# A two-layer trunk on one core: the work between dense blocks gathered into runs, one pool of eight PSUM banks, joined inverses

## The chip, the core and the metric

The kernel runs on one core of one Trainium2 chip. The metric is device time in microseconds of one execution. The core has a matrix engine (TensorE, PE in the profile), a vector engine (VectorE, DVE), an activation engine (ScalarE, ACT), GpSimd (POOL) and SyncE (SP), which issues most transfers. Each engine takes its own instructions in order and waits on semaphores for the others.

## What is computed

A sequence of 256 tokens of width 2048 goes through two layers. Layer 0 is differential attention and a gated MLP with a depthwise convolution (ffn); layer 1 is a gated delta net and a second ffn. Cut to what matters:

```python
x = x + diff_attention(rms_norm(x, mixer_norm[0]), ...)      # 8 heads, two scores each
x = x + conv_ffn(rms_norm(x, ffn_norm[0]), ...)              # 2048 -> 2 x 5504 -> 2048
x = x + gated_deltanet(rms_norm(x, mixer_norm[1]), ...)      # 16 key heads, 32 value heads
x = x + conv_ffn(rms_norm(x, ffn_norm[1]), ...)

# inside the delta net, per head and chunk of 64 tokens
low = where(strict, einsum(k_beta, k) * decay, 0)
a_mat = low + eye(64)
u = triangular_solve(a_mat, v_beta); w = triangular_solve(a_mat, k_beta * exp(g_c))
v_new = u - w @ state;  o = q_dec @ state + qk @ v_new
```

All of it is float32 in and out.

## The kernel before

Tokens lie along the free dimension, features along the 128 partitions. A product with a weight matrix is a **dense block**: `dense` (L109) makes 256 output features from all input features in chunks of four 128-row tiles. For each chunk `weights` (L85) loads 512 KB of weights (`raw`, on SP), casts them on ACT to a rounded copy (`whi`, L98), and takes the rest on DVE (`wlo`, L99). Each tile then makes three passes on PE (L123 to L125): high by high, low by high, high by low. `dense_tok` (L178) does the same with tokens on the partitions, in passes of 512 columns (L190), in chunks of two tiles.

The **other work** (normalization, scores, transposes, the delta rule) is written as Python generators. `spawn` puts one into the list `bg`; after each chunk of a dense block `tick` (L80) advances every generator to its next `yield`. That sets a priority only: the scheduler of the program then places each instruction, by a simulated timeline of its own, where it finds it ready, so a step of other work may stand anywhere among the dense passes.

PSUM is split into two pools: `dps` with two tiles of two banks each for dense blocks (`ps`), and `mps` with four banks for the rest (`mp`).

The delta net handles its 16 key heads in four blocks of four, b = 0 to 3. Per block it runs four key projections, one value projection, two gate projections by `dense_tok` (`z`), and three more value projections; behind those come the output projections `out` of the block before. `keys` makes for each head the sum of squares (`mp<-qp,onesr`, L284), scales and exponents on ACT, the product of norms on DVE (`cv<-cv,qs`, L567), and then the products k·k and k·q (`mp<-cv`, L574 and L575), from which come `lt` and `qkt`. When all four heads are there, `invert` (L589) inverts 32x32 triangles of the whole block on DVE: a transpose to `X` (L594), 30 steps of two dependent operations (L602 and L605), and two transposes to `ttc` and `tcc` (L609, L611). `levels` (L614) joins the 32x32 inverses to 64x64 ones on PE in small tiles, in four steps, each fed by copies out of PSUM; it does so for two heads at a time, inside `group` (L670). `group` then applies the rule and makes the activations `oc` for `out`. `gates` (L784) makes the decays once, in a chain of small operations from `mp<-fold,glin` to `mp<-gt,con`.

Attention sums squares of queries and keys (`mp<-sqp,onesr`, L284), makes scores (`mp<-qkn`, L411 and L412) and weights their values.

Of the kernel before, what the change touches and what calls it, by code (L numbers as in the profile page):

```python
# [13 lines left out]
PSUM = bass.MemoryType.PSUM  # L14
DATA = mybir.DependencyInfo(mybir.DependencyClass.Sync, mybir.DependencyReason.DATA)
# [9 lines left out]
RING = 4  # L25
LNEXP = "natural_log_exp_and_others"


class Trunk:
# [8 lines left out]
    def __init__(self, ctx, tc):  # L38
        self.tc, self.nc = tc, tc.nc
        nc = self.nc  # L40
        self.bg = deque()
        self.cp = ctx.enter_context(tc.tile_pool(name="cp", bufs=1))
# [15 lines left out]
        nc.scalar.preload_act_table_set(LNEXP)  # L58
# [9 lines left out]
    def mp(self):  # L68
        return self.mps.tile([P, 512], F32, tag="mp", name="mp")

    def warm(self, n):

        p = self.mp()
        for _ in range(n):
            self.nc.tensor.matmul(p[:, :P], self.ones, self.ones, start=True, stop=True)

    def spawn(self, gen):
        self.bg.append(gen)
# [6 lines left out]
    def weights(self, ap, d, pieces=1):  # L85

        nc = self.nc
        nk, n = ap.shape[1:]

        def tile_(tag, dt, bufs, room=0, d=0):  # L90
            t = self.wp.tile([P, CK * T + room], dt, tag=tag, name=tag, bufs=bufs)
            return t[:, d:d + nk * n].rearrange("p (k n) -> p k n", n=n)

        raw, hi, lo = tile_("raw", F32, RING), tile_("whi", F32R, RING, P, d), tile_("wlo", F32R, RING, P, d)
        for i in range(pieces):
            s = slice(i * nk // pieces, (i + 1) * nk // pieces)
            self.load = nc.sync.dma_start(raw[:, s, :], ap[:, s, :])
            self.cast = nc.scalar.copy(hi[:, s, :], raw[:, s, :])  # L98
            nc.vector.tensor_tensor(lo[:, s, :], raw[:, s, :], hi[:, s, :].bitcast(F32), ALU.subtract)  # L99
        return hi, lo  # L100
# [5 lines left out]
    def banks(self):  # L106
        return self.dps.tile([P, 2, 2 * T], F32, tag="ps", name="ps")

    def dense(self, w, kt, acts, place, tiles=2):  # L109
# [3 lines left out]
        for k0, nk in self.chunks(kt, CK):  # L113
            hi, lo = self.weights(w[:, k0:k0 + nk, :], (place - GAP) % P)
            steps = [(k, c) for k in range(nk) for c in range(tiles)]
            if k0 + nk == kt:
                steps = [(k, c) for c in range(tiles) for k in range(nk)]
            for k, c in steps:
                a = acts(k0 + k)
                first, last = k0 + k == 0, k0 + k == kt - 1  # L120
                s = slice(c * P, (c + 1) * P)
                o = ps[:, c, :T]
                nc.tensor.matmul(o, hi[:, k, s], a[:, 0, :], start=first, stop=False)  # L123
                nc.tensor.matmul(o, lo[:, k, s], a[:, 0, :], start=False, stop=False)  # L124
                nc.tensor.matmul(o, hi[:, k, s], a[:, 1, :], start=False, stop=last)  # L125
# [7 lines left out]
    def twin(self, w, kt, acts, place):  # L133
# [3 lines left out]
        for k0, nk in self.first_chunks(kt):  # L137
            for k in range(k0, k0 + nk):
                acts(k)
            hi, lo = self.weights(w[:, k0:k0 + nk, :], (place - GAP) % P, 1 if k0 else nk)  # L140
# [5 lines left out]
            for l, i, k, c in steps:  # L146
                nc.tensor.matmul(pss[c // 2][:, c % 2, :T], l[:, k, c * P:(c + 1) * P], acts(k0 + k)[:, i, :],  # L147
# [8 lines left out]
    def dense_gate(self, w, kt):  # L156

        nc = self.nc
        ps = self.banks()
        n = w.shape[2]  # L160
        for k0, nk in self.chunks(kt, CK):
# [8 lines left out]
            for k in range(nk):  # L170
                a = self.h[k0 + k]
                passes = [(2 * n, both[:, k].rearrange("p i n -> p (i n)"), a[:, 0, :]), (n, both[:, k, 0, :], a[:, 1, :])]
                for m, l, r in passes if k0 + k == 0 else passes[::-1]:
                    nc.tensor.matmul(ps[:m, 0, :T], l, r, start=k0 + k == 0 and m > n, stop=k0 + k == kt - 1 and m > n)
# [3 lines left out]
    def dense_tok(self, w, kt, acts):  # L178
# [3 lines left out]
        for k0, nk in self.chunks(kt, CK // 2):  # L182
            hi, lo = self.weights(w[:, k0:k0 + nk, :], HP + LEAD)
            for k in range(nk):
                a = acts(k0 + k)
                first, last = k0 + k == 0, k0 + k == kt - 1
                for c in range(2):
                    ah, al = (a[:, i, c * P:(c + 1) * P] for i in range(2))
                    for j, (l, r) in enumerate(((ah, hi), (ah, lo), (al, hi))):
                        nc.tensor.matmul(ps[:, c, :], l, r[:, k, :], start=first and not j, stop=last and j == 2)  # L190
# [33 lines left out]
    def norm_stat(self, parts=(KD, KD), switch=False):  # L224
# [10 lines left out]
        nc.tensor.matmul(ps[:, :T], self.ones, ss, start=True, stop=True)  # L235
        for c in range(2):
            last = nc.tensor.matmul(
# [41 lines left out]
    def total(self, out, parts):  # L279

        n = len(parts)
        for i, p in enumerate(parts):
            for j in range(2):
                last = self.nc.tensor.matmul(out, self.onesr, p[:, j], start=i + j == 0, stop=i + j == n)  # L284
        return last

    def add_out(self, blk, ps, done):

        x = self.x[:, 2 * blk:2 * blk + 2, :]
        self.nc.vector.tensor_tensor(x, ps[:, :, :T], x, ALU.add)  # L290
# [5 lines left out]
    def project(self, w, kt, acts, place, done, final=False):  # L296

        n = KD // 2
        for b in range(n):
# [4 lines left out]
            for c in range(2):  # L304
                k = 2 * b + c
                self.nc.vector.tensor_tensor(self.x[:, k, :], ps[:, c, :T], self.x[:, k, :], ALU.add)
# [30 lines left out]
    def attention(self, w_first, w_qk, w_v, w_o, nh, dist_ap, ident_ap, qg, kg, lvec, sub, start, done, lambda_init):  # L337

        nc, mp = self.nc, self.mp
        with self.tc.tile_pool(name="at", bufs=1) as at:  # L340
# [9 lines left out]
            def prepare():  # L350
                for _ in range(11):
                    yield
                with self.tc.issue_after(self.load.ins):
                    nc.sync.dma_start(dist, dist_ap)
                    nc.sync.dma_start(ident, ident_ap)
                nc.vector.tensor_scalar(qgs, qg, P ** -0.5, None, ALU.mult)
                nc.vector.tensor_scalar(subs, sub, 1.0 - lambda_init, None, ALU.mult)
                for i in range(2):
# [623 lines left out]
```

## Time and profile before

| | us |
|---|---|
| median of 3 runs (lowest, highest) | 2635.81 (2635.53, 2636.52) |
| the profiled execution's own time | 2635.23 |
| its span, first to last instruction | 2633.4 |
| VectorE busy in the span | 1840.9 |
| ScalarE busy in the span | 1451.2 |
| TensorE's mean granted clock | 1.000 |

The times of one instruction are rows of the trace. Matmuls overlap, and their ends are modelled: what one costs is the distance between the starts of two that follow each other, not its own length. A float32 matmul has two records, a float32r one or a transpose has one. A row of a group gives busy time and mean time of one, then the idle time of its engine just ahead of it, with what ended that.

### The profile page before, as it was taken

How to read it: one execution, taken by the hardware profiler on the slowest of the kernel's cores; microseconds unless marked ns; L12 is line 12 of the kernel's file. 1: busy time of each engine (PE TensorE's matmuls, PEld its weight loads, DVE VectorE, ACT ScalarE, POOL GpSimd, SP SyncE). 2: the span in 40 equal slices, each digit the busy share in tenths (PEclk: the TensorE clock that was granted, in tenths of full speed). 3: DMA queues.
4: the chain of work that ended last, by engine and by line, in shares of the span. 5: the costliest groups of instructions: out<-in, count | busy, mean ns of one | idle time of the engine just before them, and what ended most of it. 6: DMA issues, size and time to landing. Idle time of an engine off the chain costs nothing.

```text
span 2633.4 us, 53599 instructions
## 1 busy us (share of the span) xinstructions
PE 2625.5 (100%) x22324; PEld 2566.1 (97%) x22324; DVE 1840.9 (70%) x2716; ACT 1451.2 (55%) x1996; POOL 92.9 (4%) x188
## 2 busy tenths in 40 slices
PE   9999999999999999999999999999999999999999
PEld 9998899999999999999989989989999999999999
DVE  7876567777777555589788688688677777776444
ACT  6665555555555444485674674674555555554333
POOL 0000000000000000011011011021000000000000
PEclk9999999999999999999999999999999999999999
DMA  7555566666666666655455365455466666666665
GB/s 247 162 175 174 156 199 195 194 193 196 194 194 194 193 193 194 193 179 193 137 184 187 125 195 169 150 184 177 138 195 194 195 194 194 194 194 199 199 202 152
DMA packets 138244, 485.34 MB, mean 184 GB/s; under 512 B 15728, under 2 KB 19088, under 8 KB 138000
## 3 DMA queue, kind: packets, MB, share of 16 engines
q1 hardware_dynamic: 137712, 481.56, 59.3%
q8 instruction: 174, 2.85, 0.4%
q14 instruction: 70, 0.57, 0.1%
q10 hardware_dynamic: 288, 0.35, 0.0%
HBM read 479.72 MB, written 2.13 MB: 183 GB/s over the span
## 4 chain that ended last, share of the span: by engine, by line
PE 99%; DVE 0%; DMA 0%; ACT 0%; issue 0%; SPq 0%; DVEq 0%
PE ps L123 27%; PE ps L124 27%; PE ps L125 27%; PE ps L190 10%; PE mp L687 2%; PE ps L147 1%; PE mp L284 1%; PE mp L575 1%; PE mp L657 0%; PE mp L651 0%; PE mp L666 0%; PE mp L574 0%; PE mp L412 0%; PE mp L442 0%; PE mp L731 0%; DMA raw<-w_first 0%
## 5 line engine op out<-in xcount | busy, mean ns | idle before, releaser
L99 DVE TENSOR_TENSOR wlo<-raw,whi 128x1024 fp32r<-128x1024 f32 (+1 forms) x905 | 1102.6, 1220 | 616.4 <-ACT whi L98 613.3
L98 ACT CAST whi<-raw 128x1024 fp32r<-128x1024 f32 (+1 forms) x905 | 944.9, 1046 | 987.3 <-PE ps L125 825.1
L123 PE MATMUL ps<-h,whi 128*128 128x256 f32 x4224 | 1171.9, 277 | 0.0
L125 PE MATMUL ps<-h,whi 128*128 128x256 f32 x4224 | 1171.7, 277 | 0.0
L124 PE MATMUL ps<-h,wlo 128*128 128x256 f32 x4224 | 1171.6, 277 | 0.0
L124 PEld LDWEIGHTS ps<-h,wlo 128*128 128x128 f32 x4224 | 793.8, 188 | 1.3
L123 PEld LDWEIGHTS ps<-h,whi 128*128 128x128 f32 x4224 | 793.7, 188 | 1.2
L125 PEld LDWEIGHTS ps<-h,whi 128*128 128x128 f32 x4224 | 793.8, 188 | 0.5
L123 PE MATMUL ps<-ac,whi 128*128 128x256 f32 x1632 | 451.2, 277 | 0.0
L124 PE MATMUL ps<-ac,wlo 128*128 128x256 f32 x1632 | 451.2, 277 | 0.0
L125 PE MATMUL ps<-ac,whi 128*128 128x256 f32 x1632 | 451.1, 277 | 0.0
L124 PEld LDWEIGHTS ps<-ac,wlo 128*128 128x128 f32 x1632 | 306.5, 188 | 0.0
L123 PEld LDWEIGHTS ps<-ac,whi 128*128 128x128 f32 x1632 | 306.5, 188 | 0.0
L125 PEld LDWEIGHTS ps<-ac,whi 128*128 128x128 f32 x1632 | 306.4, 188 | 0.0
L190 PE MATMUL ps<-whi,h 128*128 128x512 f32 x768 | 240.8, 390 | 0.0
L190 PEld LDWEIGHTS ps<-whi,h 128*128 128x128 f32 x768 | 144.2, 188 | 29.8
L190 PE MATMUL ps<-wlo,h 128*128 128x512 f32 x384 | 150.1, 391 | 0.0
L123 PE MATMUL ps<-oc,whi 128*128 128x256 f32 x512 | 143.0, 279 | 0.8 <-ACT oc L734 0.8
L125 PE MATMUL ps<-oc,whi 128*128 128x256 f32 x512 | 142.8, 279 | 0.6 <-DVE oc L735 0.6
L124 PE MATMUL ps<-oc,wlo 128*128 128x256 f32 x512 | 142.8, 279 | 0.0
L265 DVE SCALAR_TENSOR_TENSOR cv<-u,fcols,cv 128x255 f32<-128x255 f32 (+1 forms) x344 | 142.8, 477 | 0.0
L131 DVE TENSOR_TENSOR u<-ps,rstd 128x512 f32<-128x512 f32 x118 | 81.4, 690 | 36.3 <-PE ps L125 35.3
(205 smaller groups left out, 2069.2 us busy)
## 6 DMA issues: line engine op xcount, KB each, us to landing
raw<-w_up SPq DMA_DIRECT2D x344, 512.0 KB, 4.3
raw<-w_down SPq DMA_DIRECT2D x160, 512.0 KB, 3.7
raw<-w_in SPq DMA_DIRECT2D x128, 512.0 KB, 4.4
raw<-w_z SPq DMA_DIRECT2D x64, 512.0 KB, 3.9
raw<-w_out SPq DMA_DIRECT2D x64, 512.0 KB, 4.2
raw<-w_qk SPq DMA_DIRECT2D x56, 512.0 KB, 4.1
raw<-w_v SPq DMA_DIRECT2D x32, 512.0 KB, 3.7
raw<-w_o SPq DMA_DIRECT2D x32, 512.0 KB, 4.4
```

What stands on the lines that cost most here:

```text
L98: self.cast = nc.scalar.copy(hi[:, s, :], raw[:, s, :])
L99: nc.vector.tensor_tensor(lo[:, s, :], raw[:, s, :], hi[:, s, :].bitcast(F32), ALU.subtract)
L123: nc.tensor.matmul(o, hi[:, k, s], a[:, 0, :], start=first, stop=False)
L124: nc.tensor.matmul(o, lo[:, k, s], a[:, 0, :], start=False, stop=False)
L125: nc.tensor.matmul(o, hi[:, k, s], a[:, 1, :], start=False, stop=last)
L131: self.nc.vector.tensor_tensor(u, ps[:, :, :T], self.rstd.unsqueeze(1).to_broadcast([P, 2, T]), ALU.mult)
L147: nc.tensor.matmul(pss[c // 2][:, c % 2, :T], l[:, k, c * P:(c + 1) * P], acts(k0 + k)[:, i, :], start=k0 + k == 0 and l is hi and i == 0, ...
L190: nc.tensor.matmul(ps[:, c, :], l, r[:, k, :], start=first and not j, stop=last and j == 2)
L265: nc.vector.scalar_tensor_tensor(out[:, j:], u[:, :T - j], taps[n - 1 - j], out[:, j:], ALU.mult, ALU.add)
L284: last = self.nc.tensor.matmul(out, self.onesr, p[:, j], start=i + j == 0, stop=i + j == n)
L575: nc.tensor.matmul(p[:, P:384], k[:, :P], r, start=True, stop=True)
L687: nc.tensor.matmul(p[:, v, :], l(v), r[:, v, :], start=i == 0, stop=i == len(terms) - 1)
```

## The change

Four things are done.

- **Runs.** A generator may `yield RUN`. `tick` now counts; generators at a plain `yield` go on at every tick, those at `RUN` only at every `period`-th. The period is 4, one dense block of four chunks; it is 1 in attention's output projection, and 2 in the first and last block of the delta net outside the key projections. Where it is 4, all PE work that a tick issues is chained (`queue`): each matmul is ordered behind the one before it, the first behind the last dense pass, and the next dense pass behind the last of the run.
- **Banks.** One pool of eight banks, used in turn; a dense block takes two of them as two tiles, so that evictions (`merge`, `add_out`) are two operations, one for each.
- **Joined inverses.** `levels` becomes `join`: it works once for all four heads of a block, behind `invert`, and its steps are steps of runs. `group` waits until the block is joined, and until the group before has got two steps on. `keys` of a head wait for those of the head before.
- **Start and ends.** Six warm matmuls instead of nine; the first loads are cut up and spread over SP's and ACT's queues, the first weights cast on DVE; small loads of attention come at other ticks.

```diff
     def tick(self):
-        for g in list(self.bg):
-            if next(g, self) is self:
-                self.bg.remove(g)
+        self.ticks += 1
+        slot = self.ticks % self.period == 0
+        for run in (False, True):
+            self.run = run and self.period == CK
+            for task in list(self.bg):
+                if task[1] is (RUN if run else None) and (slot or not run) and task[2:] != [self.ticks]:
+                    task[1:] = [next(task[0], self), self.ticks]
+                    if task[1] is self:
+                        self.bg.remove(task)
+        self.run = False
+    def queue(self, ins):
+        if self.run or self.resume:
+            self.tc.add_manual_dep(ins.ins, self.last.ins.name, ORDER)
+            self.resume = self.run
+        self.last = ins
+        return ins
-        self.dps = ctx.enter_context(tc.tile_pool(name="dps", bufs=2, space=PSUM))
-        self.mps = ctx.enter_context(tc.tile_pool(name="mps", bufs=4, space=PSUM))
+        self.ps = ctx.enter_context(tc.tile_pool(name="ps", bufs=8, space=PSUM))
     def banks(self):
-        return self.dps.tile([P, 2, 2 * T], F32, tag="ps", name="ps")
+        return [self.bank("ps") for _ in range(2)]
     def merge(self, ps, u):
-        self.nc.vector.tensor_tensor(u, ps[:, :, :T], self.rstd.unsqueeze(1).to_broadcast([P, 2, T]), ALU.mult)
+        for c in range(2):
+            self.nc.vector.tensor_tensor(u[:, c, :], ps[c][:, :T], self.rstd, ALU.mult)
...
             def keys(hq, c, cc, b0, res):
+                while "col" not in gates or turn[0] < hq:
+                    yield
...
-                yield
-                yield
+                turn[0] = hq + 1
+                yield RUN
                 prods = []
...
-                inv += [ttc, tcc]
+                yield from join(lqs, ttc, tcc, mark)
+            def join(lqs, ttc, tcc, mark):
+                while using:
+                    yield
...
+                yield RUN
                 pp = small(32)
-                for m in range(nm):
+                for m in every:
                     for s in (0, 2):
-                        nc.tensor.matmul(pp[quad[s + 1], m, :], lview[m // 2][quad[s], m % 2, quad[s + 1]],
-                                         tcc[quad[s], m0 + m, :], start=True, stop=True)
+                        self.mm(pp[quad[s + 1], m, :], lt(m)[quad[s], quad[s + 1]],
+                                         tcc[quad[s], m, :], start=True, stop=True)
...
+                yield RUN
                 px = small(32)
...
             def group(gi, gr, lqs, mark, vt, ready, zts, acts):
-                while len(inv) < 2:
+                while mark not in joined or len(ready) < len(gr) or gi and steps.get((mark, gi - 1), 0) < 2:
                     yield
-                yield from levels(TT, Ta, [lt for lt, _ in sub], *inv, 4 * gr[0])
...
                 for op, i in plan + [("v", i) for i in range(1, hb)]:
+                    self.period = 2 if op != "k" and b in (0, nb - 1) else CK
```

Matmuls are now issued in one line of the kernel, L78, and transposes in L81, so the rows of PE are told apart by their tiles. The first place in the order is PE at b=1, from the last key's products to the first step of the join. Before, with L123 to L125 and L190 for the dense passes:

```order
L575 MATMUL mp<-cv 128x256
L666 MATMUL mp<-con,cv 128x128 x4
L190 MATMUL ps<-whi,h 128x512 x2
...
L125 MATMUL ps<-oc,whi 128x256
L630 MATMUL mp<-tcc,lt 32x32 x16
L123 MATMUL ps<-oc,whi 128x256
```

And after the change:

```order
L78 MATMUL mp<-cv 128x256
L81 MATMUL mp<-con,cv 128x128 x4
L78 MATMUL ps<-whi,h 128x512
...
L78 MATMUL ps<-whi,h 128x512
L78 MATMUL mp<-tcc,lt 32x32 x32
L78 MATMUL ps<-h,whi 128x256
```

Between the rows shown stood 528 dense passes of 256 columns and 40 of 512; now there stand 137 of 512. At b=2 there are 144, at b=0 and b=3 192 (all of 512 columns). On DVE, between `X` and `tcc`, stand all 60 operations of the 30 steps, and with them 11 casts of weights (`wlo`) at b=1 now, 12 at b=2, 15 at b=0 and b=3; before, there were 19 to 23 casts and 12 to 18 operations of convolutions.

The second place is PE at b=0, the first steps of the join. Before, 29 dense passes stood between the first step (`mp<-tcc,lt`) and the second (`mp<-ttc,pc`), and 38 from there to the third (`mp<-Ta,lt`). After the change:

```order
L78 MATMUL ps<-whi,h 128x512
L78 MATMUL mp<-tcc,lt 32x32 x32
L78 MATMUL mp<-ttc,pc 32x32
L78 MATMUL mp<-pc,TT 32x32 x8
L78 MATMUL mp<-ttc,pc 32x32 x31
L78 MATMUL mp<-pc,TT 32x32 x8
L78 MATMUL mp<-Ta,lt 64x64 x8
L78 MATMUL ps<-h,whi 128x256
```

The three steps follow each other without a dense pass.

The third place is PE at b=0, the sums of squares of the last key head and its products. Before:

```order
L190 MATMUL ps<-whi,h 128x512
L284 MATMUL mp<-qp,onesr 128x512
L190 MATMUL ps<-whi,h 128x512
...
L190 MATMUL ps<-whi,h 128x512 x2
L574 MATMUL mp<-cv 128x128
L575 MATMUL mp<-cv 128x256
```

And after the change:

```order
L78 MATMUL mp<-qp,onesr 128x512
L78 MATMUL ps<-h,whi 128x256
L78 MATMUL mp<-qp,onesr 128x512
L78 MATMUL mp<-cv 128x128
L78 MATMUL mp<-cv 128x256
```

The products stood 49 dense passes behind the second sum; now they follow it directly. In the same way the two places of the gates' chain (`mp<-fold,glin` and `mp<-gt,con`) had 192 dense passes between them and have 114, and the eight sums of the first two heads of attention, which stood in eight places, are one row, `mp<-sqp,onesr 128x512 x8`, behind the fifth dense block (480 passes).

More of the change, by code (lines that the diff above doesn't have):

```diff
@@ L25 @@
 RING = 4
+RUN = "run"
 LNEXP = "natural_log_exp_and_others"
@@ L68, in mp, with bank, mm, tr @@
     def mp(self):
-        return self.mps.tile([P, 512], F32, tag="mp", name="mp")
+        return self.bank("mp")
+    def bank(self, name):
+        return self.ps.tile([P, 2 * T], F32, tag="bank", name=name)
+    def mm(self, *args, **kwargs):
+        return self.queue(self.nc.tensor.matmul(*args, **kwargs))
+    def tr(self, *args, **kwargs):
+        return self.queue(self.nc.tensor.transpose(*args, **kwargs))
+    def queue(self, ins):
[4 more added lines that the diff above has]
+        return ins
     def warm(self, n):
@@ L74, in warm @@
         for _ in range(n):
-            self.nc.tensor.matmul(p[:, :P], self.ones, self.ones, start=True, stop=True)
+            self.mm(p[:, :P], self.ones, self.ones, start=True, stop=True)
     def spawn(self, gen):
-        self.bg.append(gen)
+        self.bg.append([gen, None])
     def tick(self):
-        for g in list(self.bg):
-            if next(g, self) is self:
-                self.bg.remove(g)
-    def weights(self, ap, d, pieces=1):
-        nc = self.nc
[L88 to L99, printed above, removed]
+        self.ticks += 1
@@ new lines, in fetch, with weights @@
+    def fetch(self, ap):
+        raw = self.part(ap, "raw", F32, RING)
+        self.load = self.nc.sync.dma_start(raw, ap)
+        return raw
+    def weights(self, ap, d, raw=None, cast=None):
+        nc = self.nc
+        raw = self.fetch(ap) if raw is None else raw
+        hi, lo = self.part(ap, "whi", F32R, RING, P, d), self.part(ap, "wlo", F32R, RING, P, d)
+        if cast:
+            cast(hi, lo)
+            return hi, lo
+        self.cast = nc.scalar.copy(hi, raw)
+        self.low = nc.vector.tensor_tensor(lo, raw, hi.bitcast(F32), ALU.subtract)
@@ L121, in dense @@
                 s = slice(c * P, (c + 1) * P)
[L122 to L125, printed above, removed]
+                o = ps[c][:, :T]
+                self.mm(o, hi[:, k, s], a[:, 0, :], start=first, stop=False)
+                self.mm(o, lo[:, k, s], a[:, 0, :], start=False, stop=False)
+                self.mm(o, hi[:, k, s], a[:, 1, :], start=False, stop=last)
             self.tick()
@@ L129, in merge, with first, cast, twin @@
     def merge(self, ps, u):
-        self.nc.vector.tensor_tensor(u, ps[:, :, :T], self.rstd.unsqueeze(1).to_broadcast([P, 2, T]), ALU.mult)
-    def twin(self, w, kt, acts, place):
+        for c in range(2):
+            self.nc.vector.tensor_tensor(u[:, c, :], ps[c][:, :T], self.rstd, ALU.mult)
+    def first(self, ap, d, raw, acts):
+        nc = self.nc
+        def cast(hi, lo):
+            for i in range(2):
+                s = slice(i * T, (i + 1) * T)
+                nc.vector.tensor_copy(hi[:, 0, s], raw[:, 0, s])
+            for k in range(raw.shape[1]):
+                acts(k)
+                if k:
+                    nc.scalar.copy(hi[:, k, :], raw[:, k, :])
+                nc.vector.tensor_tensor(lo[:, k, :], raw[:, k, :], hi[:, k, :].bitcast(F32), ALU.subtract)
+        return self.weights(ap, d, raw, cast)
+    def twin(self, w, kt, acts, place, raw, ahead):
         nc = self.nc
@@ L158, in dense_gate @@
         nc = self.nc
-        ps = self.banks()
+        ps = self.bank("ps")
         n = w.shape[2]
@@ L189, in dense_tok @@
                     for j, (l, r) in enumerate(((ah, hi), (ah, lo), (al, hi))):
-                        nc.tensor.matmul(ps[:, c, :], l, r[:, k, :], start=first and not j, stop=last and j == 2)
+                        self.mm(ps[c], l, r[:, k, :], start=first and not j, stop=last and j == 2)
             self.tick()
@@ L234, in norm_stat @@
         ps = self.mp()
-        nc.tensor.matmul(ps[:, :T], self.ones, ss, start=True, stop=True)
+        self.mm(ps[:, :T], self.ones, ss, start=True, stop=True)
         for c in range(2):
-            last = nc.tensor.matmul(
+            last = self.mm(
                 ps[:, T + c:T + c + 1], ss[:, c * P:(c + 1) * P], self.ones[:, :1], start=True, stop=True)
@@ L283, in total @@
             for j in range(2):
-                last = self.nc.tensor.matmul(out, self.onesr, p[:, j], start=i + j == 0, stop=i + j == n)
+                last = self.mm(out, self.onesr, p[:, j], start=i + j == 0, stop=i + j == n)
         return last
     def add_out(self, blk, ps, done):
-        x = self.x[:, 2 * blk:2 * blk + 2, :]
-        self.nc.vector.tensor_tensor(x, ps[:, :, :T], x, ALU.add)
+        for c in range(2):
+            x = self.x[:, 2 * blk + c, :]
+            self.nc.vector.tensor_tensor(x, ps[c][:, :T], x, ALU.add)
         if done:
@@ L522, in gdn @@
             gates = {}
+            turn, steps = [0], {}
             def lin(ps):
```

263 lines of the change are left out of this document (148 added, 115 removed).

## The prediction

> **What bounds the kernel now.** I read the page first: the busy row and the chain of work that ended last.
>
> ```profile
> PE 2625.5 (100%) x22324; PEld 2566.1 (97%) x22324; DVE 1840.9 (70%) x2716; ACT 1451.2 (55%) x1996; POOL 92.9 (4%) x188
> PE 99%; DVE 0%; DMA 0%; ACT 0%; issue 0%; SPq 0%; DVEq 0%
> ```
>
> The chain is TensorE (PE) almost from end to end, and no other engine has 1% of it. So nothing that VectorE (DVE) or ScalarE (ACT) does now ends late, and whatever makes PE wait is added to the time in full. The next view is busy time by windows: a stretch of layer 0's ffn, and the stretch in which block b=1 of the delta net inverts its matrices.
>
> ```profile
> core 0: us, PE busy (x) PEld busy (x) DVE busy (x) ACT busy (x) POOL busy (x), PEclk, DMA share, GB/s
> 700.00:800.00 100.00, 100.00 (x885) 100.00 (x884) 71.96 (x101) 55.41 (x75) 0.00 (x0) 1.00 0.64 193
> 1364.70:1430.60 65.90, 65.90 (x554) 64.76 (x553) 62.04 (x114) 32.21 (x38) 1.75 (x6) 1.00 0.57 185
> ```
>
> The dense passes of 256 columns start 100 / 882 = 0.1134 us apart (three of the 885 only reach into the window). The second row matters most: there DVE is busy 62.0 of 65.9 us. It has no slack, and PE is not held up only because nothing in PE's queue needs the inverse yet. The dense work does not change (19,312 passes of 256 columns and 1152 of 512, with 16 narrow ones), so the question is what happens between its blocks.
>
> **What the change saves.** Gathering the other work leaves 100 stretches of it between dense passes where there were 161, and 16 stretches of 32x32 and 64x64 tiles where there were 28. The timeline of PE shows what a stretch of small tiles costs to enter and leave.
>
> ```profile
> 1244.97 0.28 PE L123 MATMUL ps<-h,whi 128*128 128x256 f32 x1
> 1245.17 0.69 PE L630 MATMUL mp<-tcc,lt 32*32 32x32 f32 x32
> 1245.80 0.39 PE L124 MATMUL ps<-h,wlo 128*128 128x256 f32 x1
> 1246.02 0.28 PE L125 MATMUL ps<-h,whi 128*128 128x256 f32 x1
> ```
>
> The first small matmul starts 0.20 us behind a dense one that takes 0.113, and the dense pass behind the stretch holds its successor off for 0.22 instead of 0.113: 0.2 us for each. Twelve fewer are worth 2.4 us. A single transpose shows the price of a stretch at full size.
>
> ```profile
> 1291.47 0.28 PE L123 MATMUL ps<-h,whi 128*128 128x256 f32 x1
> 1291.59 0.27 PE L731 MATMUL mp<-con,zt 128*128 128x128 f32 x1
> 1291.82 0.28 PE L125 MATMUL ps<-h,whi 128*128 128x256 f32 x1
> ```
>
> Two dense passes and the transpose take 0.35 us, of which 0.227 is dense. The 0.12 left is hardly more than the 0.11 of a transpose among others (the row of eight below), so I put the other 49 at 0.02 each, 1 us. [...]
>
> ```profile
> 1886.00 1.04 PE L731 MATMUL mp<-con,zt 128*128 128x128 f32 x8
> 1887.89 0.38 PE L123 MATMUL ps<-oc,whi 128*128 128x256 f32 x1 [0.85 <-ACT oc L734]
> ```
>
> Here the last `out` waits for its activations, about 1.9 us with what follows; the new ends of the last block have dense passes in that place. The new start (three warm matmuls fewer, loads over two queues) and the two-part evictions I put at 1.7 us together, between 0 and 3. **Saved: 7 us, between 3 and 10.**
>
> **The joined inverse, b=1 and b=2.** The rule of a bound run is a wait: PE takes its instructions in order, and everything dense stands behind the run. In the order, the last key's products (`mp<-cv`) and the first step of the join (`mp<-tcc,lt`) had 568 dense passes between them at b=1 (528 of 256 columns, 40 of 512), 69 us. After the change there are 137 of 512 columns (144 at b=2). Their spacing, and the work of DVE that must fit:
>
> ```profile
> 1364.84 0.61 PE L190 MATMUL ps<-whi,h 128*128 128x512 f32 x2
> ...
> 1368.24 0.61 PE L190 MATMUL ps<-whi,h 128*128 128x512 f32 x2
> ```
>
> ```profile
> L99 DVE TENSOR_TENSOR wlo<-raw,whi 128x1024 fp32r<-128x1024 f32 (+1 forms) x905 | 1102.6, 1220 | 616.4 <-ACT whi L98 613.3
> L605 DVE TENSOR_TENSOR Ti<-Ti,tmp 128x30 f32<-128x30 f32 (+14 forms) x120 | 39.6, 330 | 2.3
> L602 DVE TENSOR_TENSOR tmp<-X,Ti 128x30 f32<-128x30 f32 (+14 forms) x120 | 39.4, 328 | 2.4
> L611 DVE STREAM_TRANSPOSE tcc<-Ti 128x1024 f32<-128x1024 f32 x4 | 8.7, 2185 | 0.0
> L609 DVE STREAM_TRANSPOSE ttc<-Ti 128x1024 f32<-128x1024 f32 x4 | 8.4, 2102 | 0.1
> ```
>
> Fifteen passes in 3.40 us are 0.227 us each, so PE comes to the join 137 x 0.227 = 31.1 us after the products (32.7 at b=2). DVE needs, for one inverse, (39.6 + 39.4 + 8.7 + 8.4) / 4 = 24.0 us, 1.25 for `X` (below) and some 0.7 for the negated copy of a tile of that size: 26.0. Between `X` and `tcc` its order holds 11 casts of weights (12 at b=2) of 1.22 us, 13.4 (14.6). Ahead of `X` stand the products of the last key, the copies into `Cc` and two casts:
>
> ```profile
> 1360.30 0.38 PE L574 MATMUL mp<-cv 128*128 128x128 f32 x2
> ...
> 1364.76 1.25 DVE L594 STREAM_TRANSPOSE X<-Cc 128x1024 f32<-128x1024 f32 x1 [0.61 <-POOL Cc L585]
> ```
>
> That is 4.5 us. Together 43.9 against 31.1, and 45.1 against 32.7: 12.8 and 12.4, and I take **14 at each, 28**, since the 60 steps depend on each other and the latency between them is in no group's busy time. Bounds: nothing if all casts rode in gaps of the inverse (4.5 + 26.0 are 30.5); with the 65.9 us that `X` to `tcc` took in before, 39 each.
>
> **b=0 and b=3.** Here 192 passes, 43.6 us, stand between products and join, and 15 casts: 4.5 + 26.0 + 18.3 make 48.8, a wait of 5.2, taken as 6.5 for the same latency. Behind the first step the order has the next two with no dense pass between, each fed by copies out of PSUM.
>
> ```profile
> L633 DVE COPY pc<-mp 32x256 f32<-32x256 f32 x8 | 3.3, 418 | 0.2
> ```
>
> The copies have twice the elements now; two in turn for `pc` and one for `Ta` at about 0.65 are 2 us. **17 us** for both blocks, between 4 and 40.
>
> **The gates.**
>
> ```profile
> 1112.52 0.56 PE L796 MATMUL mp<-fold,glin 128*128 128x64 f32 x4
> ...
> 1132.77 0.29 DVE L816 SCALAR_TENSOR_TENSOR gt<-gt,ga 128x32 f32<-128x32 f32 x2
> ```
>
> The chain of small operations from the fold to the last `gt` takes 20.5 us among the casts and convolutions. PE now meets its product after 114 dense passes, 12.9 us, instead of 192. It waits 7.6 us if the chain keeps its length; **6** with fewer casts in between; bounds 0 and 8.
>
> **Keys.** At b=0 the sum of squares of the last key and its products now stand next to each other; the trace shows what lies between.
>
> ```profile
> 1170.42 0.39 PE L284 MATMUL mp<-qp,onesr 128*128 128x512 f32 x1
> ...
> 1171.00 1.28 ACT L252 ACT_TABLE_LOAD   x1
> ...
> 1180.12 0.69 DVE L567 TENSOR_TENSOR cv<-cv,qs 128x512 f32<-128x512 f32 x1
> ```
>
> As it ran, 10.4 us, about half of it casts and convolutions that need not stand there; the table load and the product alone are 2.0. I take **6** at b=0 and 6 at b=3, where the same pair meets, and **4** at b=2, where two sums stand behind products whose squares are still being made: 16 us, between 6 and 25.
>
> **Attention.** All eight sums of the first two heads now stand at the end of the fifth dense block, which PE passes at about 65.9 us.
>
> ```profile
> 67.60 0.63 ACT L276 CAST sqp<-sq 128x512 fp32r<-128x512 f32 x1
> ...
> 69.05 0.68 DVE L277 TENSOR_TENSOR sqp<-sq,sqp 128x512 fp32r<-128x512 f32 x1
> ```
>
> The last of these squares is split at 69.7 us now, so 3.8 us of waiting at least; **5** with the first heads' scaling ahead of it. The transposes of `zt` that are no longer spread I put at **2**.
>
> **The clock.** PE's warm-up rows and the last window show the granted clock move.
>
> ```profile
> 1.05 4.21 PE L75 MATMUL mp<-ones 128*128 128x128 f32 x18 [1.05 <-DVE eps L50]
> 1482.62 1.05 PE L687 MATMUL mp<-w,lt 128*128 128x128 f32 x8
> 2633.60:2634.00 0.40, 0.00 (x0) 0.00 (x0) 0.00 (x0) 0.00 (x0) 0.00 (x0) 0.50 0.00 0
> ```
>
> The same shape goes at 0.23 us a record for the first 4.2 us and at half of that later, and the clock is 0.50 some 4 us after the last matmul. A wait of 4 to 7 us may drop it, one of 14 surely does, and 4 us at half rate lose 2. Nine waits are that long: between 4 and 18 us, taken as **10**. [...]
>
> **The sum.** Waits 28 + 17 + 6 + 16 + 5 + 2 = 74. Against the profiled execution's own 2635.2 us: + 74 + 10 - 7 = 2712; its time is 0.6 below the median of the runs, inside the rounding. I predict 2712 us, 2.9% slower.
>
> **Rivals.** (1) *The joined work is ready in time*: the run waits for nothing and only the savings are left, 2635 - 7 = 2628. It decides at 31 us for `X` to `tcc` and what precedes it. For it: DVE could do the inverse before the casts that stand between. Against it: the order has the casts in between, and without them 30.5 of the 31.1 us are already taken. 4%, and 2% more that smaller waits cancel the savings. (2) *Only the inverses wait* because the shorter chains are faster without the casts around them: 2635 + 45 + 5 - 7 = 2678. 7%. (3) *The ring of eight banks stops dense blocks*: a block now takes the two banks given out longest ago, and a group that still reads `os` in one of them holds up both the block and all behind it; eight groups at about 2 us are 16 more, 2728. No bank is waited for in the trace of before. 9%. (4) *The clock stays up*, 2702, 14%, or falls at each wait and the waits last longer, 2725, 14%. The forecast itself, 50%.
>
> **Range and chances.** The bounds of the long terms do not add up at one end; forecast, (3) and (4) lie within 2690 to 2735, 87%, and I keep that. Faster by over 0.2% (about what a measurement of this kernel can tell from no change): 0.04. Within it: 0.02. Slower: 0.94.
>
> **What would show it.** Right: idle time of PE ahead of `mp<-tcc,lt` of 12 to 17 us at b=1 and b=2, released by the transposes on DVE; 5 to 7 us ahead of the gates' product and of `mp<-cv` at b=0; a mean granted clock below 1.00 behind them. Wrong: `tcc` done before PE comes to the join, DVE idle in these stretches, or idle time of PE ahead of `ps` that ends with an eviction.

## The result and the profile after

| | before | after |
|---|---|---|
| median (lowest, highest), us | 2636.16 (2635.53, 2637.39) | 2724.23 (2723.21, 2725.75) |
| span of the profiled execution, us | 2633.4 | 2721.4 |
| TensorE's mean granted clock | 1.000 | 0.983 |

The ratio is 1.0335, with a 95% interval of 1.0322 to 1.0348: the kernel is 88 us slower. The page after, busy times and the chain that ended last:

```profile
PE 2648.0 (97%) x22318; PEld 2584.6 (95%) x22318; DVE 1856.9 (68%) x2903; ACT 1444.7 (53%) x1988; POOL 76.2 (3%) x188
PE 94%; DVE 4%; ACT 1%; issue 1%; DMA 0%; SPq 0%; DVEq 0%; ACTq 0%
```

PE is busy in 97% of its span instead of all of it, and DVE has appeared in the chain. PE idles 73.4 us where it idled 7.9; and it is busy 22.5 us longer with six records fewer. Two things were lost, then: time in waits, and speed. What ended PE's waits (engine and line that waits, what it waited for, us in total, times, the longest):

```profile
PE mp L78 <- DVE tcc L680: 36.3, 4, 14.5
PE mp L78 <- DVE cv L636: 10.7, 2, 6.0
PE mp L78 <- DVE gt L898: 5.8, 1, 5.8
PE mp L78 <- ACT sqp L333: 5.4, 1, 5.4
PE mp L78 <- DVE qp L334: 3.8, 2, 2.4
PE mp L78 <- ACT qp L333: 2.2, 2, 1.8
PE mp L78 <- DVE pc L712: 1.5, 2, 0.8
PE mp L78 <- DVE Ta L725: 1.2, 2, 0.6
...
PE mp L81 <- DVE zt L803: 0.7, 2, 0.6
```

These are 67.6 us, all of them ahead of `mp`, the other work; no dense block waits for a bank. More than half are the joins. Two of the four, on the timeline of PE:

```profile
1419.64 1.56 PE L78 MATMUL mp<-tcc,lt 32*32 32x32 f32 x51 [14.53 <-DVE tcc L680]
1646.22 1.92 PE L78 MATMUL mp<-tcc,lt 32*32 32x32 f32 x64 [13.27 <-DVE tcc L680]
```

The speed is seen in a table of windows, cut to the nine stretches in which the granted clock stood at half:

```profile
67.10:73.90 6.80, 3.63 (x13) 3.10 (x14) 4.58 (x9) 4.84 (x8) 0.00 (x0) 0.50 0.21 72
...
1237.80:1251.50 13.70, 11.95 (x198) 11.62 (x199) 3.42 (x6) 2.07 (x5) 5.20 (x10) 0.50 0.14 41
1408.50:1425.60 17.10, 5.96 (x83) 5.92 (x84) 10.93 (x25) 0.58 (x1) 5.67 (x13) 0.50 0.10 32
...
1865.90:1879.60 13.70, 12.12 (x199) 11.79 (x200) 3.34 (x6) 2.07 (x5) 4.17 (x9) 0.50 0.14 41
sum 92.40, PE 54.36 PEld 50.36 DVE 47.64 ACT 24.82 POOL 24.64; mean PE 6.04 PEld 5.60 DVE 5.29 ACT 2.76 POOL 2.74
```

The first number behind the length is PE's busy time. Each of the nine lies on or behind one of the long waits, and PE worked 54.4 us in them. If all of that goes at half rate, 27 us are lost. Small tiles of 32x32 took 28 ns a record at 0.50 and 17 at 1.00 in a probe (below), less than twice as long; with that for the small tiles of the join I estimate the loss at about 25. 67.6 + 25 is 92.6, against 88.1: about 4.5 us were saved elsewhere, by this account.

### The profile page after: what moved, and what is told of

Read it like the earlier page. It is cut to its first block, busy times and chain, and to the rows that moved or that the text cites. A ratio compares the mean times of both kernels' runs of the same rounds, so it can differ in the third digit from the quotient of the medians.

```text
span 2721.4 us, 53724 instructions
## 1 busy us (share of the span) xinstructions
PE 2648.0 (97%) x22318; PEld 2584.6 (95%) x22318; DVE 1856.9 (68%) x2903; ACT 1444.7 (53%) x1988; POOL 76.2 (3%) x188
## 4 chain that ended last, share of the span: by engine, by line
PE 94%; DVE 4%; ACT 1%; issue 1%; DMA 0%; SPq 0%; DVEq 0%; ACTq 0%
PE ps L78 88%; PE mp L78 5%; DVE wlo L134 1%; PE mp L81 1%; ACT whi L133 0%; DVE cv L322 0%; DVE Ti L674 0%; DVE tcc L680 0%; DVE tmp L671 0%; DMA raw<-w_in 0%; DMA raw<-w_first 0%; DVE d L624 0%; DVE ttc L678 0%; ACT L309 0%; DVE u L167 0%
## 5 line engine op out<-in xcount | busy, mean ns | idle before, releaser
L78 PE MATMUL ps<-h,whi 128*128 128x256 f32 (+1 forms) x8608 | 1486.5, 278 | 1.5 <-DVE whi L176 1.1
L78 PEld LDWEIGHTS ps<-h,whi 128*128 128x128 f32 (+1 forms) x8608 | 1306.5, 189 | 3.7 <-issue 1.3
L78 PE MATMUL ps<-h,wlo 128*128 128x256 f32 x4288 | 1181.7, 278 | 0.0
L78 PEld LDWEIGHTS ps<-h,wlo 128*128 128x128 f32 x4288 | 806.1, 189 | 1.4 <-issue 0.2
L78 PE MATMUL ps<-ac,whi 128*128 128x256 f32 x3264 | 555.9, 276 | 0.0
L78 PEld LDWEIGHTS ps<-ac,whi 128*128 128x128 f32 x3264 | 492.2, 188 | 0.0
L78 PE MATMUL ps<-ac,wlo 128*128 128x256 f32 x1632 | 450.2, 276 | 0.0
L78 PEld LDWEIGHTS ps<-ac,wlo 128*128 128x128 f32 x1632 | 306.3, 188 | 0.0
L78 PE MATMUL ps<-whi,h 128*128 128x512 f32 x768 | 242.5, 393 | 0.0
L78 PE MATMUL ps<-oc,whi 128*128 128x256 f32 x1024 | 179.0, 278 | 0.0
L78 PEld LDWEIGHTS ps<-whi,h 128*128 128x128 f32 x768 | 145.7, 190 | 31.0
L78 PEld LDWEIGHTS ps<-oc,whi 128*128 128x128 f32 x1024 | 155.7, 188 | 0.0
L78 PE MATMUL ps<-wlo,h 128*128 128x512 f32 x384 | 150.5, 392 | 0.0
L78 PE MATMUL ps<-oc,wlo 128*128 128x256 f32 x512 | 141.3, 276 | 0.0
L167 DVE TENSOR_TENSOR u<-ps,rstd 128x256 f32<-128x256 f32 x236 | 98.3, 420 | 8.3 <-PE ps L78 0.9
L78 PEld LDWEIGHTS ps<-oc,wlo 128*128 128x128 f32 x512 | 96.2, 188 | 0.0
L320 ACT ACTIVATE cv<-u,fcols 128x256 f32<-128x256 f32 x172 | 93.6, 592 | 0.0
L78 PEld LDWEIGHTS ps<-wlo,h 128*128 128x128 f32 x384 | 73.0, 190 | 15.3
L322 DVE SCALAR_TENSOR_TENSOR cv<-u,cols,cv 128x255 f32<-128x255 f32 (+2 forms) x192 | 82.8, 475 | 1.3 <-ACT cv L318 1.1
```

Source lines behind the costliest of these rows:

```text
L78: return self.queue(self.nc.tensor.matmul(*args, **kwargs))
L167: self.nc.vector.tensor_tensor(u[:, c, :], ps[c][:, :T], self.rstd, ALU.mult)
L320: nc.scalar.activation(out, u, AF.Identity, bias=bias, scale=taps[n - 1])
L322: nc.vector.scalar_tensor_tensor(out[:, j:], u[:, :T - j], taps[n - 1 - j], out[:, j:], ALU.mult, ALU.add)
```

## The experiments

Each kernel was run beside the kernel before the change (2635.6 to 2635.9 us). Ratios are to it, with 95% intervals.

### Edges or banks

The prediction put the waits down to the bound runs. That has two parts that can be undone one by one: the order edges between the matmuls of a run, and the one pool of eight banks. First, the edges are left out.

```diff
-            self.run = run and self.period == CK
+            self.run = False
```

> The order edges between the matmuls of a run are left out; the slots, the joined inverses and the one pool of eight banks stay. Theory A (the prediction's: the bound run is the wait, since everything dense stands behind it): with no edges dense passes go ahead of work that is not ready, so the 69.5 us of waits of the changed kernel and the 23 us at half clock behind them go: 2724 - 92 = 2632, between 2628 and 2645. Theory B (the ring: a dense block takes the banks given out longest ago, so it cannot be brought ahead of work whose banks were given out before its own): the order stays as it is, idle time ahead of mp<-tcc of 30 us or more, 2715 to 2728. Theory C (each of the two is enough by itself): as B here.

Measured: 2721.52 us, ratio 1.0331 (1.0313 to 1.0348). Waits of PE:

```profile
PE mp L78 <- DVE tcc L680: 39.3, 4, 15.4
PE mp L78 <- DVE cv L636: 11.7, 2, 6.2
PE mp L78 <- DVE gt L898: 6.0, 1, 6.0
PE mp L78 <- ACT sqp L333: 5.4, 1, 5.4
```

The same four waits lead, in the same places; only those for `qp` fell, from 6.0 to 1.1 us. Theory A falls: the edges by themselves are not what puts dense passes behind the join. Second, the edges stay and the banks are parted.

```diff
-        self.ps = ctx.enter_context(tc.tile_pool(name="ps", bufs=8, space=PSUM))
+        self.dps = ctx.enter_context(tc.tile_pool(name="dps", bufs=4, space=PSUM))
+        self.mps = ctx.enter_context(tc.tile_pool(name="mps", bufs=4, space=PSUM))
-        return self.ps.tile([P, 2 * T], F32, tag="bank", name=name)
+        pool = self.dps if name == "ps" else self.mps
+        return pool.tile([P, 2 * T], F32, tag="bank", name=name)
```

> Dense blocks get a pool of four banks and the other work one of four, as before the change in size; the edges of the runs stay. Theory A: the runs are bound as before, so nothing goes: 2718 to 2728. Theory B: dense passes may go ahead, the waits go: 2628 to 2645. Theory C: some dense blocks may go ahead where the edges leave room, but runs still wait: between 2660 and 2715, with idle time ahead of mp<-tcc.

Measured: 2690.65 us, 1.0210 (1.0195 to 1.0225).

```profile
PE mp L80 <- DVE tcc L682: 27.3, 2, 14.0
PE mp L80 <- DVE lt L651: 8.6, 5, 1.8
PE mp L80 <- DVE gt L900: 5.9, 1, 5.9
PE mp L80 <- ACT sqp L335: 5.4, 1, 5.4
```

Read the count behind the 27.3: two waits instead of four. (The five waits for `lt` are new in this run and stand ahead of sums of squares; they were not followed up.) The two that are left are those of b=1 and b=2. At b=0 and b=3 the period is 2 behind the keys, and `tick` makes edges only at a period of 4: there the ring alone had held the join in front, and with the ring gone its wait is gone. At b=1 and b=2 the edges hold it as well. Both undone:

> Both at once: two pools of four banks and no order edges. Theories A, B and C all give 2628 to 2645 here, with hardly any idle time ahead of mp<-tcc. Theory D (neither: the slots of the ticks give out the join too early, whatever the banks and edges do): idle time ahead of mp<-tcc stays above 25 us and the time above 2690. The saving of the gathered work by itself is what this run stays below 2636, if it does: 3 to 10 us by the prediction.

Measured: 2644.29 us, 1.0034 (1.0021 to 1.0047).

```profile
PE ps L80 <- DVE qkr L169: 3.2, 1, 3.2
PE mp L80 <- DVE cv L638: 2.1, 2, 1.2
PE mp L83 <- DVE zt L805: 1.1, 2, 0.8
```

No wait for `tcc` is left. So theory C holds: the ring (the eight banks given out in turn) is enough by itself at all four blocks, the edges by themselves at b=1 and b=2. Either part undone alone would have told a wrong story (edges: no effect; banks: 34 of the 80 us). The order says the same. Dense passes of the whole program that PE has behind it when it comes to the join of each block:

| | b=0 | b=1 | b=2 | b=3 |
|---|---|---|---|---|
| after the change | 9584 | 10544 | 11888 | 13232 |
| without edges | 9584 | 10544 | 11888 | 13232 |
| two pools | 9855 | 10544 | 11888 | 13466 |
| both | 9892 | 10849 | 12228 | 13572 |

That there is a turn at all does not yet say that it is the turn that stops a dense block. If it is (its banks are given out behind those of the join, so it can't be brought ahead of it), it should be enough to take the join's tiles out of the turn.

```diff
+        self.js = ctx.enter_context(tc.tile_pool(name="js", bufs=2, space=PSUM))
+    def own(self):
+        return self.js.tile([P, 2 * T], F32, tag="own", name="mp")
-                    return mp()[:, :nm * len(sets) * n].rearrange("p (m c) -> p m c", c=n)
+                    return self.own()[:, :nm * len(sets) * n].rearrange("p (m c) -> p m c", c=n)
```

(`pq` and `pz` likewise, no edges, and six banks are left for the turn.)

> The run without order edges, with one thing more: the tiles of the join (pp, px, py, pq, pz) come from two banks of their own, and all the rest, dense blocks too, takes turns in the other six. If it is the turn that stops dense blocks (a block's banks are given out behind those of the join, so it cannot go ahead of it), the waits at the joins go, 39.3 for tcc and 2.8 for pc and Ta, with some 11 us of half clock behind them, and the others stay as they are, since their tiles still stand in the turn (11.7 ahead of mp<-cv, 6.0 for the gates, 5.4 for attention): 2721.5 - 42 - 11 = 2668, between 2658 and 2685. If dense blocks need four banks of their own, whatever the turn: nothing goes, above 2705. If the joins held up everything else too: 2635 to 2650.

Measured: 2675.89 us, 1.0151 (1.0135 to 1.0168).

```profile
PE mp L82 <- DVE cv L640: 11.2, 2, 6.2
PE mp L82 <- DVE gt L902: 5.8, 1, 5.8
PE mp L82 <- ACT sqp L337: 4.3, 1, 4.3
```

The waits for `tcc` are gone, and those whose tiles still stand in the turn are as they were, to 1.1 us. That is the turn's mark, work by work. Nothing of it shows as a wait for a bank: the turn acts earlier, on the order in which PE gets its instructions.

### How long the join waits

Here the join is given out eight ticks later in the changed kernel, and nothing else is changed.

```diff
                 nc.vector.transpose(tcc.rearrange("p m c -> p c m"), t.rearrange("p i c -> p c i"))
+                for _ in range(8):
+                    yield
                 yield from join(lqs, ttc, tcc, mark)
```

> The changed kernel with the join given out eight ticks later, nothing else. Eight ticks are 8 x 24 passes of 0.1134 us or 8 x 12 of 0.227, 21.8 us of dense work, and eight casts of 1.22 us, 9.8 us of DVE. If the wait is the difference of these two lengths (the prediction's sum), each join waits 12 us less: about 2.5 of 14.5 stays at b=1, 2 of 13.7 at b=2, nothing of 4.3 and 5.0 at b=0 and b=3; with the clock that they lose, 12 us in all, the time is 2724 - 33 - 10 = 2681, between 2670 and 2692. If DVE does the transposes late in any case (their place in its order moves along with the join), the waits stay: above 2710.

Measured: 2683.59 us, 1.0182 (1.0167 to 1.0197). The waits at b=0 and b=3 are gone; these are left:

```profile
1428.75 1.46 PE L78 MATMUL mp<-tcc,lt 32*32 32x32 f32 x47 [9.06 <-DVE tcc L680]
1640.30 1.92 PE L78 MATMUL mp<-tcc,lt 32*32 32x32 f32 x64 [4.44 <-DVE tcc L680]
```

The time came out as expected, though not by the expected sum: the two waits are shorter by 5.5 and 8.8 us and not by 12. Between `X` and `tcc` DVE did more than the eight casts that were expected: at b=1 eight more casts and 8.9 us of convolutions and other work (`cv`, `u`, `oc`), at b=2 six more casts and 4.6 us. And the waits for `qp`, `pc` and `Ta` went too, 8.7 us that nobody had foreseen. The wait is a difference of two lengths, as the prediction had it, but the length on DVE grows with what is given out meanwhile.

### What the half clock costs, and what ends it

Here the waits of the joins are filled with matmuls that nobody needs, so that PE does not idle.

```diff
                 pp = small(32)
+                flat2 = pp.rearrange("p m c -> p (m c)")
+                for _ in range(14 if mark in (0, nb - 1) else 58):
+                    self.mm(flat2[:, :P], self.ones, self.ones, start=True, stop=True)
```

> The changed kernel, with float32 matmuls of ones ahead of the first matmul of each join: 14 at b=0 and b=3, 58 at b=1 and b=2, at 0.224 us each 3.1 and 13.0 us, just inside waits of 4.3, 14.9, 13.7 and 5.0. They do nothing but keep TensorE at work. If the time at half clock behind these waits (4.0, 2.1, 1.5 and 4.1 us lost) is due to TensorE's idling, it goes and nothing else changes: 2724 - 11.7 = 2712, between 2709 and 2717. If the small tiles of the joins hold the clock down by themselves, the long half clocks of b=0 and b=3 stay: 2719 or more.

Measured: 2716.16 us, 1.0306 (1.0292 to 1.0321): 8 us less than the changed kernel. That is within the first answer's 2709 to 2717, at its far end. PE's busy time at half clock fell from 54.4 to 37.6 us, half of which difference is 8.4: the idle time had cost that. But the half clock did not go everywhere. Of PE's busy time in it, 3.4 us stayed at b=0 (12.0 in the changed kernel), 3.4 at b=1 (6.0), none at b=2 (4.7), and most at b=3 (12.1):

```profile
1862.20:1872.50 10.30, 9.70 (x118) 9.47 (x112) 1.88 (x4) 1.57 (x5) 2.26 (x5) 0.50 0.26 91
```

At b=3 three waits of 1.1, 0.8 and 0.6 us were left ahead of the small tiles and among them. This is what stood behind the filler at b=1:

```profile
1417.02 1.20 PE L78 MATMUL mp<-tcc,lt 32*32 32x32 f32 x64 [1.59 <-DVE tcc L680]
...
1419.10 0.63 PE L78 MATMUL ps<-h,whi 128*128 128x256 f32 x2
1419.52 0.41 PE L78 MATMUL ps<-h,wlo 128*128 128x256 f32 x1
1419.73 0.63 PE L78 MATMUL ps<-h,whi 128*128 128x256 f32 x2
```

A wait of 1.6 us was left, and 1.2 us of small tiles behind it; from 1418.5 on three dense passes take 0.63 instead of 0.34, for one window of 3.4 us. So the second answer held at b=3 and not at b=0, and neither theory holds alone. Probes in layer 0's ffn, where PE otherwise never waits, separate the parts: copies on POOL make PE wait for a graded time, with dense passes or small tiles behind it.

```diff
+    def probe(self, fp, n, kind, count):
...
+        self.run = True
+        if n:
+            self.mm(p[:, :P], self.ones, self.ones, start=True, stop=True)
+            nc.scalar.copy(s[:, :P], p[:, :P])
+            for _ in range(n - 1):
+                nc.gpsimd.tensor_copy(s[:, :P], s[:, :P])
+            self.mm(q[:, :P], s[:, :P], self.ones, start=True, stop=True)
+        for i in range(count):
...
+        self.run = False
```

> The changed kernel with probes in layer 0's ffn, one look, read by window and not by its time. Six probes make TensorE wait for a chain of copies on POOL, of graded length, with dense passes behind them; two put 200 and 400 matmuls of 32x32 among the dense passes with no wait, one 40 of 128x128; three put 200 and 50 of 32x32 and 40 of 128x128 behind a wait. The prediction's theory: a wait below about 4 us costs itself alone, a longer one leaves dense passes at twice their 0.113 us for about 4 us, 2 us lost, whatever follows. Rival: the clock counts work, not time, and small tiles are too little of it: then the dense passes behind 200 and 400 of them are slow with no wait ahead, and behind a wait the small tiles run out the whole time at half clock without raising it, so that the dense passes behind them are slow as well.

The six waits with dense passes behind them, in the one execution that was profiled, are 0.95, 2.34, 3.41, 4.89, 6.99 and 9.86 us. The first and two more, on the timeline, and windows of PE's clock behind the first, the second and the fifth:

```profile
457.20 0.49 PE L80 MATMUL mp<-ones,pb 128*128 128x128 f32 x2 [0.95 <-POOL pb L380]
493.08 0.49 PE L80 MATMUL mp<-ones,pb 128*128 128x128 f32 x2 [2.34 <-POOL pb L380]
615.18 0.80 PE L80 MATMUL mp<-ones,pb 128*128 128x128 f32 x2 [6.99 <-POOL pb L380]
```

```profile
457.40:464.20 6.80, 6.80 (x61) 6.80 (x61) 4.87 (x8) 4.14 (x5) 0.00 (x0) 1.00 0.35 111
494.40:497.80 3.40, 3.40 (x18) 3.40 (x18) 1.23 (x1) 1.04 (x1) 0.00 (x0) 0.50 0.00 0
497.90:501.30 3.40, 3.40 (x32) 3.40 (x32) 2.64 (x5) 2.15 (x3) 0.00 (x0) 1.00 0.58 161
...
610.50:620.70 10.20, 5.52 (x26) 5.52 (x27) 1.05 (x1) 1.37 (x2) 3.85 (x13) 0.50 0.01 2
620.80:624.20 3.40, 3.40 (x32) 3.40 (x31) 2.55 (x5) 1.98 (x3) 0.00 (x0) 1.00 0.47 154
```

Behind the wait of 0.95 us the clock stayed at 1.00. Behind the one of 2.34 it stood at 0.50 for a window of 3.4 us, in which 18 passes started instead of 32, and that window began 1.3 us after the wait had ended. This wait is shorter than the prediction's "4 to 7". The 200 and 400 small tiles had gaps of 1.2 and 2.1 us of their own, which ended with no wait that the profile shows (`issue`), so that run could not say whether tiles or gaps had brought the clock down; but it shows their pace:

```profile
739.19 3.00 PE L80 MATMUL mp<-ones 32*32 32x32 f32 x177
744.32 17.56 PE L80 MATMUL mp<-ones 32*32 32x32 f32 x623 [2.13 <-issue]
```

That is 17 ns a record in the first row, at a clock of 1.00, and 28 in the second, at 0.50. It was still 0.50 behind the 17.56 us of the second row, until 767.5. The last probe has matmuls of 256 columns in place of the small ones. Their rows have no such gap:

```diff
+            if kind == 32:
+                a, b = slice(64 * (i % 2), 64 * (i % 2) + 32), slice(64 * (i % 2) + 32, 64 * (i % 2) + 64)
+            elif kind == 64:
+                a, b = slice(0, 64), slice(64, P)
+            else:
+                a, b = slice(0, P), slice(0, P)
+            self.mm(q[b, :T], self.ones[a, :kind], self.x[a, 0, :], start=True, stop=True)
```

> The changed kernel with other probes in layer 0's ffn, one look, read by window. In the first probe run TensorE stood still for 2.1 us among the 400 small tiles, so it is open whether the clock fell by the tiles or by that gap. Here 40 float32 matmuls of 256 columns each stand among the dense passes, so long that no instruction comes late: of 32x32, of 64x64 and of 128x128, first with no wait ahead, then behind a wait of 7.3 us. If the share of the array that works sets the clock: 1.00 until the 32x32 ones, 0.50 within about 7 us of them and until 3 to 7 us into the dense passes behind; the same or not for 64x64; nothing for 128x128; behind the wait 0.50 as long as the small tiles last, and 3 to 7 us for 128x128. If only gaps set it: 1.00 throughout the first three, and 3 to 7 us of 0.50 behind each wait.

```profile
452.00:460.00 8.00, 8.00 (x76) 4.23 (x77) 2.02 (x4) 1.35 (x2) 0.00 (x0) 1.00 0.50 156
460.00:468.00 8.00, 8.00 (x72) 7.28 (x69) 1.99 (x3) 2.14 (x3) 0.00 (x0) 1.00 0.06 9
...
702.50:710.00 7.50, 7.50 (x36) 3.31 (x38) 0.00 (x0) 0.00 (x0) 0.00 (x0) 0.50 0.00 0
710.00:718.00 8.00, 8.00 (x42) 3.32 (x38) 0.00 (x0) 0.00 (x0) 0.00 (x0) 0.50 0.00 0
...
820.00:830.00 10.00, 10.00 (x25) 5.25 (x24) 0.00 (x0) 0.00 (x0) 0.00 (x0) 0.50 0.01 2
...
908.00:913.00 5.00, 4.23 (x11) 3.52 (x12) 0.00 (x0) 0.00 (x0) 0.59 (x3) 0.50 0.00 0
913.20:920.00 6.80, 6.80 (x33) 6.00 (x32) 0.00 (x0) 0.00 (x0) 0.00 (x0) 1.00 0.00 0
```

A matmul has two records here. The first two rows are 40 matmuls of 32x32 with no wait ahead, up to 461.1, and the dense passes behind: 1.00. For 64x64 and 128x128 the windows from 540 to 560 and from 626 to 642 us show 1.00 as well. The rows from 702.5 are the same 32x32 behind a wait of 7.0 us: 0.50 as long as they last, 17 us. At 820 it is 64x64: 0.50 for 34 us. At 908 it is 128x128, behind a wait that ended at 909.1: 1.00 from 913.2 on, 4 us later. So in this execution the matmuls of 32x32 and 64x64 with 256 columns did not bring the clock down from 1.00, and in 17 and 34 us they did not bring it up from 0.50; nor did 17.56 us of 32x32 with 32 columns in the probe before. That fits the joins of b=0 and b=3, where three steps of small tiles stand in a row behind the wait: they have 12.0 and 12.1 us of PE work at half clock, and those of b=1 and b=2 have 6.0 and 4.7. Whether tiles of 32 columns help to bring it down stays open: in the filled kernel 1.6 us of waiting with 1.2 of such tiles behind it was enough at b=1, and why is not settled.

### A faster kernel

What is left in the kernel with two pools and no edges is mainly attention (the wait for `qkr`) and the transposes of `zt`. Two edits on it, together: attention's runs come at every second tick instead of every fourth, and the transposes of `zt` two ticks later.

```diff
-        self.ticks, self.period = 0, 4
+        self.ticks, self.period = 0, 2
...
                 yield RUN
+                yield
+                yield
                 for v0 in range(0, n, 2):
```

> Two pools of four banks and no order edges as in the third run, with two places mended that still cost there: attention's runs at every second tick instead of every fourth (its stretch ended 7 us later than before the change, with a wait of 3.2 for qkr and a half clock), and the transposes of zt two ticks behind their operands instead of one slot. If these two places hold what is left: 2644.3 - 7 - 2 = 2635, and with the smaller savings of the gathered work down to 2630. If the joined inverse and the slots cost something by themselves: above 2638.

Measured: 2629.81 us, ratio 0.9978 (0.9969 to 0.9987): 0.2% faster than before the change. Its page:

```profile
PE 2621.7 (100%) x22318; PEld 2563.5 (98%) x22318; DVE 1852.5 (70%) x2903; ACT 1447.3 (55%) x1990; POOL 91.0 (3%) x188
```

And what ended the longest of its waits:

```profile
PE ps L80 <- ACT whi L135: 2.4, 1, 2.4
```

That wait is in the start; the others add up to 2 us. Its other work stands in 150 stretches, nearly as many as the 161 of before, against 100 in the changed kernel: gathering by itself can explain little of its 6 us. The two edits gave 14.5 us where 9 were expected. No run parts them, but the traces show where it was won: by the starts of the same dense pass, 6.0 of the 13.4 us between the two profiled executions lie in attention and 7.4 in the delta net. With three more warm matmuls at the start:

```diff
-        t.warm(6)
+        t.warm(9)
```

> The faster kernel with nine warm matmuls at the start instead of six, as before the change. In its profile TensorE ends the warm ones at 4.0 us, waits 2.35 us for the first cast of a whole chunk and runs its dense passes at half rate from 11.6 to 15.0, 1.6 us lost. With three more the first dense pass comes 0.7 us later and the wait is that much shorter; if the clock then stays up, the time is 1.6 less, 2628; if the clock falls for other reasons or the loads end the wait anyway, the same 2630.

Measured: 2630.02 us, 0.9978 (0.9969 to 0.9987). In its profile the wait fell from 2.4 to 1.1 us and the clock stayed at 1.00, yet the time is the same: a miss. The clocks on record tell why. Of the eleven executions of the kernel with six warm matmuls, eight had a mean granted clock of 1.000 and took 2629.0 to 2629.9 us. Three had 0.999 and took 2631.1 to 2631.7; the profiled one, with its window at half rate from 11.6 to 15.0 us, is among these. One window of 3.4 us at half rate is worth 1.7 of 2629 us: a mean of 0.9994. So the median execution, at 1.000, had no such window, and there was no 1.6 us to win.

## Why the prediction was right, and where it was not

**The sum.** 2712 was predicted, 2724.2 measured, inside 2690 to 2735. Wait by wait most terms hold; that of b=0 and b=3 was put 6 us too high:

| term | predicted, us | measured, us |
|---|---|---|
| joined inverse, b=1 and b=2 | 28 | 27.8 (14.5 and 13.3) |
| joined inverse, b=0 and b=3, with the copies between steps | 17 | 11.2 (8.5, and 2.7 for `pc` and `Ta`) |
| gates | 6 | 5.8 |
| keys | 16 | 16.7 (10.7 for `cv`, 6.0 for `qp`) |
| attention | 5 | 5.4 |
| transposes of `zt` | 2 | 0.7 |
| waits together | 74 | 67.6 |
| clock | 10 | about 25 |
| saved | 7 | about 4.5 |

That the forecast is only 12 us off is partly luck: the waits were put 6.4 us too high and the clock some 15 too low, and the two errors offset each other in part.

The method behind the largest term is sound: PE's passes between products and join, against DVE's work in its order. At b=1 the trace after shows `X` at 1377.99 and `tcc` from 1417.59 on, 1.9 long: 41.5 us, where the prediction had 26.0 + 13.4 = 39.4 and 1.2 more for latency.

**The mis-sized term is the clock.** "Nine waits are that long: between 4 and 18 us, taken as 10." For these lengths the prediction shows the 4.2 us of the start and the 0.50 some 4 us after the last matmul; they were an estimate, since no row of before shows the clock fall behind a wait inside the program. In the changed kernel it stood at 0.50 or 0.51 on or behind all nine; in the probe it fell behind a wait of 2.34 us too. "4 us at half rate lose 2" assumed dense passes behind every wait; behind two of the joins stand small tiles, and there 12.0 and 12.1 us of PE work went at half clock. The upper bound, 18, lies below the estimate of 25 as well. Rival (4) had the clock fall at each wait, and longer waits with it, for 2725. That number is the nearest to the measured one, but only the first half of its mechanism came true: the waits were shorter than forecast, not longer.

**The step that named the cause was wrong.** "The rule of a bound run is a wait: PE takes its instructions in order, and everything dense stands behind the run." The order was read rightly, so the waits came out right; but without the edges the time was the same (2721.5). The ring of eight banks held the same order alone, and the edges held it alone at b=1 and b=2. Rival (3) had the ring, but looked for it as a wait of `ps` for an eviction. That wait doesn't occur. The ring costs nothing at a bank; it decides what PE is given next: 2721.52 with the ring alone, 2690.65 with the edges alone, 2644.29 with neither, 2724.23 with both.

**The savings.** Twelve fewer stretches of small tiles and the mended end were put at 2.4 and 1.9; no run tells these apart. The faster kernel, with 21 stretches of small tiles and without the wait at the last `out`, is 6 us below before, inside the 3 to 10. Its trace places most of the gain: in layer 0's ffn the same dense pass starts 0.9 us later than before the change (1.6 us of that kernel's start went to the half clock), and from the end of the delta net on 3.9 us earlier.

## What to carry to other kernels

When work that is not ready stands in front of work that is, ask for everything that could keep the scheduler from swapping them, and undo the parts singly and together: two sufficient causes hide each other. Here a pool that was shared in turn tied the order of all who used it, and no wait in the trace said so; banks of its own for the work that takes long to get ready (the join) took 46 us off. Price a wait of the bound engine with the slower clock behind it: here 67.6 us of waiting cost about 25 more, by estimate.

## What the hardware showed unexpectedly

- In the probe's one execution the clock fell to 0.50 behind a wait of 2.34 us and stayed at 1.00 behind one of 0.95. The faster kernel has a wait of 2.4 us at its start in the profile, with 0.50 behind it from 11.6 to 15.0 us, and only three of its eleven executions had a mean clock of 0.999; whether the other eight had that wait, no trace shows.
- The half-rate stretches were 3.4, 6.8, 10.2, 13.7 and 17.1 us long in the changed kernel and the probe: one to five times 3.42 (17.1 / 5), to 0.1 us. Those at the five longer waits of the probe begin at 494.4, 532.0, 572.9, 610.5 and 654.9 us: 37.6, 40.9, 37.6 and 44.4 us apart, 11.0, 12.0, 11.0 and 13.0 times 3.42. What sets these lengths, no run shows.
- Matmuls of 32x32 of 256 columns did not lower the clock in 8.8 us at 1.00, nor did those of 64x64 (51.9 us in all, 34 of them behind the wait, which leaves about 18), with 1.00 from 540 us on. They did not raise it either, in 17 and 34 us at 0.50, while with 128x128 behind such a wait it was 1.00 after 4 us.
